# Moving the second block's activation low parts by 32 bytes inside their buffers

## The chip, the cores and the metric

The kernel runs on one core of a Trainium2 chip. The metric is device time in microseconds (us) of one execution, from the first instruction of any engine to the last. Five engines work side by side from queues of their own and wait for each other by semaphores: TensorE (PE in the profile; its weight loads are listed apart as PEld), VectorE (DVE), ScalarE (ACT), GpSimd (POOL) and SyncE (SP, which here issues most of the weight transfers). Operands of the matrix multiply lie in the on-chip memory SBUF, 128 partitions wide; an address in this text is the byte offset within a partition, the same on all partitions.

## The reference, cut to what matters

The program computes two model blocks, one after the other, on 512 tokens of width 1024, in float32.

```python
x = first_block(x, ...)    # gated MLP mixer, RWKV mixer, 32 experts (top 2), RMS norm
x = second_block(x, ...)   # two layers, below

for i in range(2):
    mix = ssd_shortconv_layer_mixer(x, ...) if i == 0 else sliding_window_attention(x, ...)
    x = layer_norm(ALPHA * x + mix, ...)
    x = layer_norm(ALPHA * x + (silu(x @ w_gate[i]) * (x @ w_up[i])) @ w_down[i], ...)
    x = x + (p[i] @ w_ple[i]) * sigmoid(x @ w_ple_gate[i] + b[i])
```

The feed-forward width is 2816. The change touches the second block alone, and in it every product of a weight matrix with the activations.

## The kernel before, in words

**Three products for one.** A float32 number is split into a high part in the rounded float32 format F32R, which the multiplier takes in one pass, and a low part, the rest, in the same format. `split` (lines 285 to 288) makes the parts of an activation: ACT copies the source to `xh` (line 287), DVE subtracts and writes `xl` (line 288). `conv` (lines 254 to 261) does the same for a weight tile: ACT writes `whi`, DVE `wlo`. `mm3` (lines 278 to 283) then issues three matrix multiplies into one PSUM tile: `whi` with `xh` (line 281), `whi` with `xl` (line 282), `wlo` with `xh` (line 283). The first named is the stationary operand, loaded 128 columns at a time before each multiply; the second is the moving operand, streamed through.

**Tiling.** Activations lie transposed: 128 of the 1024 (or 2816) channels on the partitions, the 512 tokens along the free dimension. So a moving operand is one row of 512 float32 numbers, 2,048 bytes in a partition, or, where a layer norm is worked in two halves of the tokens (`HALVES`, line 1426), 256 numbers. A stationary operand is 128 numbers, 512 bytes. `linear` (line 290) runs over the output groups of 128 columns and, inside, over the 8 (or 6, 16) channel groups k, three multiplies each. A weight tile of 1,024 numbers per partition is loaded by SP, split by ACT and DVE, and used; seven such buffers of each part rotate.

**Where the activation parts live.** In the second block, pool `act` (line 1488) has four buffers of the tile `xh` and four of `xl`. `four` (lines 1491 and 1492) takes one of each; each holds four channel groups, 4 x 512 numbers. `pair` (lines 1494 to 1498) hands out one channel group's `xh` and `xl` at a time. An activation of 1024 channels therefore fills two `xl` tiles: channel groups 0 to 3 in one, 4 to 7 in another.

The pool lays the buffers of one name one after the other. The built program has the four `xh` buffers at 94,848, 103,040, 111,232 and 119,424 and the four `xl` buffers at 127,616, 135,808, 144,000 and 152,192: all a whole number of times 128. The second block's weight tiles lie at whole multiples of 128 too (4,096 bytes each), and so do the stationary pieces, in steps of 512 bytes.

**Order.** TensorE executes its instructions in program order. The order around the change is set by the program text and by a tile framework that inserts the waits; nothing in it depends on addresses. In the second block come, in this order: the state-space mixer with its short convolution (lines 1506 to 1772), the feed-forward layer and gate of layer 0 (`ffn_ple`, line 1825), the attention of layer 1 (lines 1893 to 2007), and `ffn_ple` again.

Other products matter for comparison. The experts (`lin`, lines 1277 to 1283) have the roles swapped: the weights `whi` and `wlo` are the moving operand, 512 wide, and the activations `exh` and `exl` the stationary one, 96 columns (384 bytes) each, one after the other in their tile. The small product for `dt` (lines 1600 to 1607) uses 16 stationary columns (64 bytes) at a time.

Of the kernel before, what the change touches and what calls it, by code (L numbers as in the profile page):

```python
# [11 lines left out]
F32R = mybir.dt.float32r  # L12
# [8 lines left out]
T = 512  # L21
# [1455 lines left out]
def second(K, out, dbg=None):  # L1477
# [10 lines left out]
    act = es.enter_context(tc.tile_pool(name="act", bufs=4, reuse_waits="tile"))  # L1488
    spare = []

    def four():
        return tuple(act.tile([128, 4, T], F32R, name=n_) for n_ in ("xh", "xl"))

    def pair():
        if not spare:
            h_, l_ = four()
            spare.extend((h_[:, i_], l_[:, i_]) for i_ in range(4))
        return spare.pop(0)
# [15 lines left out]
    for b in range(4):  # L1514
        nc.sync.dma_start(ys[b], K.yd[b * 128:(b + 1) * 128, :])
    bcw = [cols(w, j) for w in (group(2048), group(2304)) for j in range(2)]
    x4 = [four() for _ in range(2)]
    x3 = [(h_[:, i_], l_[:, i_]) for h_, l_ in x4 for i_ in range(4)]
    bc_ps = [K.mm() for _ in range(4)]
# [384 lines left out]
    for b in range(4):  # L1904
        ps = K.mm()
        bs = slice(b * 128, (b + 1) * 128)
        for k in range(DC):
            xh, xl = xs[k]
# [128 lines left out]
```

## Time and profile before

| what | value |
|---|---|
| time, median of 3 runs | 2478.95 us (2475.49 to 2479.7) |
| the profiled execution: its own time | 2484.5 us |
| the profiled execution: its span, first to last instruction | 2482.6 us |
| TensorE busy | 2390.5 us, 96% of the span |
| VectorE busy | 1618.2 us, 65% |
| ScalarE busy | 1135.6 us, 46% |
| mean granted TensorE clock | 0.986 of full speed |

How to read it. The profile's page gives busy time by engine and by group of instructions. A matrix multiply is listed with its start and a duration of about 0.39 us for 512 columns; since the next one starts before the last has drained, durations overlap, and it is the distance between starts that says how long TensorE takes for one. That distance is called the spacing below. The timeline lists starts in us with two decimals, so that a spacing is best taken over many: the last start less the first, divided by the number of steps between. The granted clock is 1.00 where TensorE runs at 2.4 GHz and 0.5 where it runs at 1.2 GHz.

### The profile page before, as it was taken

The numbers are of one execution on the slowest core, as the hardware profiler recorded it, in microseconds if no ns is written. First come the engines' busy times: TensorE is split into PE (matmuls) and PEld (weight loads), VectorE is DVE, ScalarE is ACT, GpSimd is POOL, SyncE is SP. The second block draws the span as 40 slices with busy tenths as digits, with TensorE's granted clock in tenths as the row PEclk, the third lists the DMA queues.
The fourth block names the chain that finished last, engine by engine and source line by source line (L and its number), as shares of the span: only waits on it lengthen the run. The fifth ranks groups of instructions, "written<-read, shape, count | busy, mean of one in ns | idle before, by whom it ended". The sixth has DMA issues, their size and how long they took to land.

```text
span 2482.6 us, 36164 instructions
## 1 busy us (share of the span) xinstructions
PE 2390.5 (96%) x14570; PEld 1872.2 (75%) x14570; DVE 1618.2 (65%) x2543; ACT 1135.6 (46%) x1452; POOL 231.8 (9%) x73
## 2 busy tenths in 40 slices
PE   7999999799999999889999999999999998999998
PEld 3788677576666666568878898888888678888887
DVE  4778775699999999866766473333394677333346
ACT  2633324577677777564335333232353654223233
POOL 0000000112334444400000000000000000000000
PEclk9999999899999999989999999999999999999999
DMA  7233334799999999672323323322333112323232
GB/s 250 90 108 109 102 101 176 288 353 354 361 359 359 357 356 359 235 242 86 119 80 113 124 94 102 97 91 92 102 107 107 35 35 86 102 85 109 91 98 69
DMA packets 187307, 408.39 MB, mean 164 GB/s; under 512 B 13408, under 2 KB 130704, under 8 KB 162560
## 3 DMA queue, kind: packets, MB, share of 16 engines
q1 hardware_dynamic: 175840, 383.00, 44.2%
q0 software_dynamic: 5536, 10.46, 1.8%
q10 hardware_dynamic: 5760, 12.59, 1.4%
q8 instruction: 115, 1.88, 0.3%
q14 instruction: 56, 0.46, 0.0%
HBM read 389.17 MB, written 25.21 MB: 167 GB/s over the span
## 4 chain that ended last, share of the span: by engine, by line
PE 52%; DMA 17%; DVE 3%; issue 3%; ACT 1%; POOLq 0%; SPq 0%; DVEq 0%; ACTq 0%
PE mm L282 16%; PE mm L281 16%; PE mm L283 16%; DMA yd<-ey,r 15%; PE sc L1969 1%; PE po L1977 1%; PE pt L1946 1%; DMA raw<-in_w_mix_dram 1%; DVE x L1471 1%; DVE wlo L260 1%; DVE x L1472 0%; DMA s_row<-ard 0%; PE aux L1715 0%; DVE x L1473 0%; DVE xl L288 0%
## 5 line engine op out<-in xcount | busy, mean ns | idle before, releaser
L260 DVE TENSOR_TENSOR wlo<-raw,whi 128x1024 fp32r<-128x1024 f32 (+3 forms) x461 | 756.2, 1652 | 259.5 <-ACT whi L259 258.9
L281 PE MATMUL mm<-xh,whi 128*128 128x512 f32 (+1 forms) x2264 | 833.4, 370 | 17.5 <-ACT xh L287 6.8
L259 ACT ACTIVATE whi<-raw 128x1024 fp32r<-128x1024 f32 (+3 forms) x461 | 637.4, 1403 | 463.2 <-PE mm L282 374.7
L282 PE MATMUL mm<-xl,whi 128*128 128x512 f32 (+1 forms) x2264 | 832.7, 368 | 2.1 <-DVE xl L288 1.8
L283 PE MATMUL mm<-xh,wlo 128*128 128x512 f32 (+1 forms) x2264 | 831.2, 368 | 0.6 <-DVE wlo L260 0.6
L281 PEld LDWEIGHTS mm<-xh,whi 128*128 128x128 f32 x2264 | 427.2, 190 | 96.3 <-issue 9.4
L282 PEld LDWEIGHTS mm<-xl,whi 128*128 128x128 f32 x2264 | 430.3, 190 | 72.5 <-DVE xl L288 4.0
L283 PEld LDWEIGHTS mm<-xh,wlo 128*128 128x128 f32 x2264 | 429.7, 190 | 72.5 <-issue 5.2
L1344 POOL DMA_INDIRECT yd<-ey,r x32 | 210.9, 6590 | 380.7 <-DVE ey L1343 375.8
L1283 PE MATMUL mm<-wlo,exh 128*96 128x512 f32 x496 | 198.0, 401 | 12.1 <-DVE wlo L260 12.0
L1281 PE MATMUL mm<-whi,exh 128*96 128x512 f32 x496 | 197.0, 397 | 4.8 <-ACT exh L287 2.7
L1282 PE MATMUL mm<-whi,exl 128*96 128x512 f32 x496 | 195.8, 395 | 0.0
L1841 DVE TENSOR_TENSOR l_h<-l_sg,mm 128x512 f32<-128x512 f32 x44 | 30.2, 688 | 182.6 <-PE mm L283 167.0
L1283 PEld LDWEIGHTS mm<-wlo,exh 128*96 128x96 f32 x496 | 80.4, 162 | 56.9 <-DVE wlo L260 23.3
L1281 PEld LDWEIGHTS mm<-whi,exh 128*96 128x96 f32 x496 | 80.9, 163 | 38.0 <-ACT whi L259 3.0
L1282 PEld LDWEIGHTS mm<-whi,exl 128*96 128x96 f32 x496 | 80.6, 162 | 35.1
L1282 PE MATMUL aux<-whi,ehl 128*96 128x512 f32 x256 | 100.6, 394 | 0.8 <-DVE ehl L288 0.8
L1281 PE MATMUL aux<-whi,ehh 128*96 128x512 f32 x256 | 100.6, 393 | 0.0
L1283 PE MATMUL aux<-wlo,ehh 128*96 128x512 f32 x256 | 98.4, 400 | 0.0
L287 ACT ACTIVATE xh<-l_h 128x512 fp32r<-128x512 f32 x44 | 27.2, 623 | 111.7 <-DVE l_h L1841 111.7
L1840 ACT ACTIVATE l_sg<-mm 128x512 f32<-128x512 f32 x44 | 25.8, 589 | 83.1 <-PE mm L283 83.0
L1282 PEld LDWEIGHTS aux<-whi,ehl 128*96 128x96 f32 x256 | 41.3, 161 | 19.3 <-DVE ehl L288 1.2
(570 smaller groups left out, 2546.4 us busy)
## 6 DMA issues: line engine op xcount, KB each, us to landing
raw<-in_moe_gate_dram SPq DMA_DIRECT2D x64, 1024.0 KB, 7.5
raw<-in_moe_up_dram SPq DMA_DIRECT2D x64, 1024.0 KB, 7.4
raw<-in_moe_down_dram SPq DMA_DIRECT2D x64, 1024.0 KB, 8.6
raw<-in_w_mix_dram SPq DMA_DIRECT2D x44, 512.0 KB, 3.5
raw<-in_w_ffn_gate_dram SPq DMA_DIRECT2D x44, 512.0 KB, 3.5
raw<-in_w_ffn_up_dram SPq DMA_DIRECT2D x44, 512.0 KB, 3.5
raw<-in_w_ffn_down_dram SPq DMA_DIRECT2D x40, 512.0 KB, 3.3
raw<-in_ada_w_dram SPq DMA_DIRECT2D x64, 256.0 KB, 2.7
```

The lines of the kernel that those rows point to most:

```text
L259: nc.scalar.activation(hi[:, :m], r[:, :m], AF.Copy)
L260: nc.vector.tensor_tensor(lo[:, :m], r[:, :m], hi[:, :m], op=OP.subtract)
L281: nc.tensor.matmul(ps, h, xh, start=start, stop=False)
L282: nc.tensor.matmul(ps, h, xl, start=False, stop=False)
L283: nc.tensor.matmul(ps, l, xh, start=False, stop=stop)
L287: self.nc.scalar.activation(xh, src, AF.Copy)
L1281: nc.tensor.matmul(ps, xh[:, k, :], wh, start=(k == 0), stop=False)
L1282: nc.tensor.matmul(ps, xl[:, k, :], wh, start=False, stop=False)
L1283: nc.tensor.matmul(ps, xh[:, k, :], wl, start=False, stop=(k == len(ww) - 1))
L1344: nc.gpsimd.indirect_dma_start(out=yd, out_offset=bass.IndirectOffsetOnAxis(ap=yi, axis=0), in_=y, in_offset=None, bounds_check=T - 1, oob ...
L1840: nc.scalar.activation(sg, pp["g", j], AF.Silu)
L1841: V.tensor_tensor(h, sg, pp["u", j], op=OP.mult)
```

## The change

Each `xl` tile gets 8 more numbers (32 bytes) per partition, and the part that is used begins behind them. Nothing else is edited; the `xh` tiles stay as they are.

```diff
     def four():
-        return tuple(act.tile([128, 4, T], F32R, name=n_) for n_ in ("xh", "xl"))
+        h_ = act.tile([128, 4, T], F32R, name="xh")
+        return h_, act.tile([128, 4 * T + 8], F32R, name="xl")[:, 8:].rearrange("p (i n) -> p i n", i=4)
```

What comes out in the built program: each `xl` buffer is now 8,224 bytes instead of 8,192, and the pool still puts them end to end, starting at 127,616. The buffers begin at 127,616, 135,840, 144,064 and 152,288, and what is used in them begins 32 bytes later: at 127,648, 135,872, 144,096 and 152,320. Modulo 128 that is 32, 64, 96 and 0. All tiles allocated above them move up by 4 x 32 = 128 bytes and keep their place modulo 128. `xh`, the weight tiles and everything below stay where they were. No engine gets another instruction, and none is moved. Of the 1,544 multiplies of the second block that stream an `xl` of 512 columns, 484 find it at 32 modulo 128, 272 at 64, 312 at 96 and 476 at 0; of the 544 that stream 256 columns, 144, 160, 112 and 128. In 16 multiplies (line 1912) a piece of `xl` off 0 modulo 128 is the stationary operand.

## Rows read from the trace of the kernel before

**Rows 1.** The page's first part: busy us, share of the span and number of instructions of an engine.

```profile
PE 2390.5 (96%) x14570; PEld 1872.2 (75%) x14570; DVE 1618.2 (65%) x2543; ACT 1135.6 (46%) x1452; POOL 231.8 (9%) x73
```

**Rows 2.** Busy time of each engine in stretches of the span: from 1080 us (about where the second block's products begin) to the end, and the gate and up and down products of the two feed-forward layers. Columns: stretch, its length, then for each engine busy us and instructions, the granted clock, the DMA engines' busy share and their GB/s.

```profile
1080.00:2482.60 1402.60, 1376.29 (x7172) 1145.29 (x7172) 755.68 (x1470) 522.03 (x839) 2.53 (x7) 0.99 0.30 95
1468.00:1789.00 321.00, 320.78 (x1457) 267.29 (x1456) 119.04 (x134) 89.63 (x110) 0.00 (x0) 1.00 0.32 102
2076.00:2397.00 321.00, 321.00 (x1463) 267.77 (x1462) 117.60 (x136) 89.81 (x110) 0.00 (x0) 1.00 0.30 96
```

**Rows 3.** The groups of TensorE's instructions from 1079.5 us to the end, different widths kept apart: line, operation, out<-in, shape, count, busy us and mean ns of one, and the idle time before them.

```profile
L282 PE MATMUL mm<-xl,whi 128*128 128x512 f32 x1536 | 601.0, 391 | 0.0
L283 PE MATMUL mm<-xh,wlo 128*128 128x512 f32 x1536 | 600.9, 391 | 0.0
...
L282 PE MATMUL mm<-xl,whi 128*128 128x256 f32 x544 | 156.3, 290 | 2.1 <-DVE xl L288 1.8
L283 PE MATMUL mm<-xh,wlo 128*128 128x256 f32 x544 | 155.2, 288 | 0.0
```

**Rows 4.** The timeline of TensorE, 512 columns, in a long undisturbed sequence: start us, length, line, tiles. The last row shown is the 24th start after the first.

```profile
1339.33 0.39 PE L281 MATMUL mm<-xh,whi 128*128 128x512 f32 x1
1339.56 0.39 PE L282 MATMUL mm<-xl,whi 128*128 128x512 f32 x1
1339.78 0.39 PE L283 MATMUL mm<-xh,wlo 128*128 128x512 f32 x1
...
1344.77 0.39 PE L281 MATMUL mm<-xh,whi 128*128 128x512 f32 x1
```

**Rows 5.** The same for 256 columns; the last row is the 26th start after the first.

```profile
1438.23 0.28 PE L281 MATMUL mm<-xh,whi 128*128 128x256 f32 x1
...
1441.35 0.28 PE L283 MATMUL mm<-xh,wlo 128*128 128x256 f32 x1
```

**Rows 6.** The timeline of TensorE just behind a foreign product (line 1765, two plain float32 multiplies) that broke into a sequence of 512 columns. The row at 1348.36 is the 9th start after the one at 1346.28, the one at 1349.72 the 6th after that.

```profile
1345.12 1.10 PE L1765 MATMUL aux<-s_v,cst_c 128*128 128x512 f32 x2
1345.65 0.79 PE L282 MATMUL mm<-xl,whi 128*128 128x512 f32 x1
1346.28 0.39 PE L283 MATMUL mm<-xh,wlo 128*128 128x512 f32 x1
1346.51 0.40 PE L281 MATMUL mm<-xh,whi 128*128 128x512 f32 x1
1346.74 0.40 PE L282 MATMUL mm<-xl,whi 128*128 128x512 f32 x1
1346.98 0.39 PE L283 MATMUL mm<-xh,wlo 128*128 128x512 f32 x1
1347.20 0.39 PE L281 MATMUL mm<-xh,whi 128*128 128x512 f32 x1
...
1348.36 0.39 PE L283 MATMUL mm<-xh,wlo 128*128 128x512 f32 x1
...
1349.72 0.39 PE L283 MATMUL mm<-xh,wlo 128*128 128x512 f32 x1
```

**Rows 7.** The same for 256 columns, behind a layer norm's two products (line 1457). The row at 1444.65 is the 7th start after the one at 1443.83.

```profile
1443.20 0.67 PE L1457 MATMUL aux<-l_q,cst_c 128*128 128x256 f32 x2
...
1443.83 0.28 PE L282 MATMUL mm<-xl,whi 128*128 128x256 f32 x1
...
1444.65 0.28 PE L283 MATMUL mm<-xh,wlo 128*128 128x256 f32 x1
```

**Rows 8.** The timeline of TensorE in the experts, 512 moving columns, 96 stationary ones. The last row is the 23rd start after the first.

```profile
706.17 0.39 PE L1281 MATMUL mm<-whi,exh 128*96 128x512 f32 x1
706.40 0.39 PE L1282 MATMUL mm<-whi,exl 128*96 128x512 f32 x1
...
711.51 0.40 PE L1281 MATMUL mm<-whi,exh 128*96 128x512 f32 x1
```

**Rows 9.** The timeline of TensorE in the product for `dt`, 512 moving columns, 16 stationary ones. The last row is the 20th start after the first.

```profile
1107.50 0.40 PE L281 MATMUL mm<-xh,wdh 128*16 128x512 f32 x1
...
1112.14 0.40 PE L283 MATMUL mm<-xh,wdl 128*16 128x512 f32 x1
```

**Rows 10.** Two lines of plain float32 products with 512 moving columns: count, duration in ns (least, median, most), first and last start, form. The moving tile `s_xde` lies at 64 modulo 128 in the built program, `o_sq` at 96.

```profile
L1726 PE MATMUL aux<-s_xde,s_bt x12: 590/592/697, 1196.8 to 1289.6; 128*128 128x512 f32 x12
L808 PE MATMUL aux<-o_sq,cst_c x8: 590/592/697, 220.3 to 375.3; 128*128 128x512 f32 x8
```

**Rows 11.** DVE's writes of the low parts of the feed-forward activations (line 288), and a DVE operation of the same width whose output `s_so` lies at 64 modulo 128 (line 1677); columns as in rows 10.

```profile
L288 DVE TENSOR_TENSOR xl<-l_h,xh x44: 681/686/694, 1481.2 to 2394.3; 128x512 fp32r<-128x512 f32 x44
L1677 DVE TENSOR_TENSOR s_so<-mm,s_so x8: 691/692/693, 1174.8 to 1313.0; 128x512 f32<-128x512 f32 x8
```

## The prediction

> **What bounds the kernel now.** I read the page's first part first: TensorE is busy 96% of the span, no other engine over 65% [rows 1]. Then the table by stretches: from 1080 us to the end TensorE is busy 1376.3 of 1402.6 us, and in the two feed-forward stretches practically all of 321 us each, at a granted clock of 1.00, while VectorE and ScalarE are at little over a third and a quarter and the DMA engines at 0.3 [rows 2]. So in the second block the time is the number of multiplies times the distance between their starts; a nanosecond more or less on each is paid in full but for the 26.3 us (2%) in which TensorE idles. The groups of TensorE give the numbers: 1,536 low-part products of 512 columns and 544 of 256, each one of a triple [rows 3].
>
> The spacing is therefore the thing to read. In a long sequence 24 steps take 1344.77 - 1339.33 = 5.44 us, 226.7 ns each [rows 4]; with 256 columns 26 steps take 3.12 us, 120.0 ns each [rows 5]. The difference is 106.7 ns for 256 columns, which is one column per period at 2.4 GHz. So 512 columns stream in 213.3 ns, 256 in 106.7, and in both cases 13.3 ns are added: exactly the time of 32 columns, or 128 bytes of the moving operand. A remainder that is the same for both widths and just 128 bytes long smells of a memory that is served in turns of 128 bytes.
>
> Two more readings say that this remainder is not fixed. Behind a foreign product the spacing first wanders between 0.22 and 0.24 us: 9 steps take 2.08 us, 231.1 ns each; only then does it settle, 6 steps in 1.36 us, 226.7 ns [rows 6]. With 256 columns the unsettled spacing is shorter: 7 steps in 0.82 us, 117.1 ns [rows 7]. And it never settles in the experts, where the stationary pieces are 384 bytes and so begin alternately at even and odd multiples of 128: 23 steps in 5.34 us, 232.2 ns [rows 8]; nor in the small product with stationary pieces of 64 bytes: 20 steps in 4.64 us, 232.0 ns [rows 9]. The settled 226.7 ns is thus found where every operand begins at the same place modulo 512 from one multiply to the next. The three unsettled values, 231.1, 232.2 and 232.0, have the mean 231.8.
>
> [...]
>
> **The change part by part.** Removed: nothing. Added: no instruction, no wait, no transfer; the order on every queue is the same. Moved: addresses.
>
> Tiles above the pool shift by 128 bytes and keep their place modulo 128; I cost that at nothing. DVE's writes of `xl` now begin off a multiple of 128: at 0 modulo 128 they take 686 ns in the median, a like operation with its output at 64 takes 692 [rows 11]. Six ns on the 44 writes of rows 11 are 0.3 us, on all low parts of the block well under 1 us, on an engine busy 755.7 of 1402.6 us [rows 2]: nothing. If that cover were gone it would still be under 1 us.
>
> What counts is the moving operand of line 282. The title's place, 32 modulo 128, holds for one of the four buffers only; the others are at 64, 96 and 0. So 1,068 of the low-part products of 512 columns are shifted and 476 are not; of those of 256 columns 416 and 128. No row shows an F32R stream that begins off a multiple of 128, so the cost is bounded from both sides. Upwards: the shifted product and its two neighbours never settle, and the spacing goes from 226.7 to 231.8 ns, 5.1 ns for each multiply. Downwards: the remainder of one multiply per triple vanishes, 13.3 ns less.
>
> I take the unsettled value, since rows 8 and 9 are nearest: there, too, one operand begins at a changing place, and the spacing stays high. The sum:
> - 512 columns: 1,068 shifted triples x 3 = 3,204 multiplies x 5.1 ns = +16.3 us.
> - 256 columns: 416 x 3 = 1,248 multiplies x (117.1 - 120.0 = -2.9 ns) = -3.6 us.
> - Triples with `xl` at 0 stand among shifted ones: a product over 8 channel groups takes 12 multiplies from one tile and 12 from the next, and settling takes 9 (rows 6). So up to three quarters of them stay unsettled: 476 x 3 x 0.75 x 5.1 ns = +5.5 us, less 128 x 3 x 0.75 x 2.9 ns = 0.8 us.
>
> That is +12.7 us without the last item and +17.4 us with all of it. A few of these multiplies are unsettled already, behind foreign products, and some fall where TensorE idles anyway, so I stay near the lower end: +14 us. A second way to the same size: if starts are bound to turns of 128 bytes, a shift of 64 makes the way there 16 columns longer than a whole turn and the way back too, 48 + 48 + 32 instead of 32 + 32 + 32, which is 32 columns or 13.3 ns per triple; on 1,068 triples +14.2 us. The profiled execution took 2484.5 us, which would become 2498.5; it lies 5.5 us above the median of the runs, 2478.95. On that median the forecast is 2493.
>
> **The rivals.**
>
> Nothing happens. Plain float32 products of 512 columns have the same least and median duration, 590 and 592 ns, whether their moving tile lies at 64 or at 96 modulo 128 [rows 10]. If F32R streams are as indifferent, the spacing stays at 226.7 and 120.0 ns and the time at 2479, between 2474 and 2484. Against it: the same remainder reacts to where stationary pieces begin [rows 8, 9], and a float32 product of 512 columns takes 590 ns where an F32R one takes 391 [rows 3], so that its memory has more time for each column. [...] Chance 0.27.
>
> Faster: the turns help. If the next stream may begin as soon as its own turn comes and needs less than 8 columns of a gap, then going from `xh` to a shifted `xl` and back costs one turn of 32 columns together where it now costs two. Each shifted triple loses 13.3 ns: (1,068 + 416) x 13.3 = -19.8 us, 2459. It speaks for it that the remainder is 32 columns for either width. Against it: among 512 columns no spacing in rows 6 is under 0.22 us, while this needs 0.217 regularly. It decides from the point where a shift of 8 columns is enough for the gap. This is the case on the other side. Chance 0.17.
>
> Slower by much more: not only the shifted triples but all 1,536 of 512 columns stay unsettled, 4,608 x 5.1 = +23.5 us, and the 256 wide ones gain nothing: 2502. It is the upper end of the forecast's own range, not a case apart.
>
> That the change does not do what it says is built in: three of the four buffers lie elsewhere than at 32. Were it the 32 alone that matters, only 484 of the 512 wide triples would pay, 484 x 3 x 5.1 = +7.4 us, 2486, the lower end of the forecast's own range.
>
> **How the numbers follow.** Slower by unsettled streams 0.56 (own range 2486 to 2504), nothing 0.27, faster 0.17. What a measurement of this kernel can tell from no change is about 0.2%, 5 us; the case "nothing" lies within it, so the three chances are the same three numbers. The range that leaves out the faster case and a little of the upper tail goes from 2473 to 2504.
>
> **What will show it.** In the timeline of the feed-forward stretches, 512 columns: a spacing averaged over 24 starts of about 231 to 232 ns says that the forecast's step is right, 226.7 the first rival, about 222 the second. With 256 columns: 117 against 120 ns. The counts of all engines and the DMA rows should be as before, and the granted clock 1.00 in these stretches. I am wrong if the two stretches of 321 us are not longer; if they are longer by about 3 us each, the step is right, since their 1,457 instructions are some 485 triples [rows 2] of which 69% are shifted (1,068 of 1,544): 485 x 0.69 x 3 x 5.1 ns = 5.1 us each, and 3 us if a good third of them settle. It would also be wrong if the time came from elsewhere, say from longer `xl` writes on VectorE that TensorE waits for.

## The result and the profile after

The changed kernel takes 2498.67 us in the median of 4 runs (2495.5 to 2502.66), the kernel before 2478.34 in the same comparison: a ratio of 1.0085, 95% interval 1.0072 to 1.0099, so 20.3 us more (18 to 25 by the interval). The profiled execution after took 2499.61 us, its span is 2497.7 us.

The page's first part after, against [rows 1]: the same number of instructions on every engine, 16 us more in TensorE's multiplies, 6 us less in its weight loads (PEld), under 1 us of difference elsewhere.

```profile
PE 2406.9 (96%) x14570; PEld 1866.6 (75%) x14570; DVE 1617.5 (65%) x2543; ACT 1135.3 (45%) x1452; POOL 231.6 (9%) x73
```

The stretches of [rows 2] after (stretch, its length, then busy us and instructions of each engine, granted clock, DMA share, GB/s): TensorE is as busy and its clock as high as before, but in 321 us of the first feed-forward layer it gets through 1,424 instructions where it was 1,457, and VectorE and ScalarE do less beside it, since they work at TensorE's pace. The third stretch lies at the same times as before, but the wide multiplies of the second layer now begin 7 us later in it (2094.44 against 2087.43 us), behind more of the narrow ones, so its count is nearly the same.

```profile
1080.00:2497.70 1417.70, 1389.90 (x7127) 1135.66 (x7125) 752.03 (x1465) 517.48 (x830) 1.55 (x2) 1.00 0.30 93
1468.00:1789.00 321.00, 320.28 (x1424) 260.98 (x1423) 115.52 (x130) 87.45 (x106) 0.00 (x0) 1.00 0.31 96
2076.00:2397.00 321.00, 321.00 (x1460) 263.05 (x1460) 118.29 (x148) 87.38 (x109) 0.00 (x0) 1.00 0.31 93
```

TensorE's groups after, against [rows 3] (line, operation, out<-in, shape, count, busy us and mean ns of one, idle time before them). Both views begin at 1079.5 us; the second block begins earlier in this trace, and some 14 of its triples of 256 columns fall before the view, which is why their counts are lower. The mean duration of the wide multiplies rises by 3 to 5 ns, that of the narrow ones falls by 4: the two widths answer with opposite signs.

```profile
L282 PE MATMUL mm<-xl,whi 128*128 128x512 f32 x1536 | 608.8, 396 | 0.0
L283 PE MATMUL mm<-xh,wlo 128*128 128x512 f32 x1536 | 605.7, 394 | 0.0
L282 PE MATMUL mm<-xl,whi 128*128 128x256 f32 x530 | 150.5, 286 | 1.2 <-DVE xl L288 1.1
L283 PE MATMUL mm<-xh,wlo 128*128 128x256 f32 x531 | 149.2, 284 | 0.0
```

The starts say it exactly. Two timelines of TensorE follow (start us, length, line, tiles), six rows of each kernel at the same places of the program: the first multiply of the `dt` product, the first and the last of the 1,416 multiplies of 512 columns that run without a break through the feed-forward layer of layer 0, two of 256 columns right behind them that are 72 steps apart, and the last multiply of all. Before:

```profile
1106.49 0.41 PE L281 MATMUL mm<-xh,wdh 128*16 128x512 f32 x1 [1.00 <-ACT wdh L287]
...
1478.66 0.50 PE L281 MATMUL mm<-xh,whi 128*128 128x512 f32 x1 [0.22 <-ACT l_sg L1840]
...
1799.55 0.39 PE L283 MATMUL mm<-xh,wlo 128*128 128x512 f32 x1
1799.78 0.28 PE L281 MATMUL mm<-xh,whi 128*128 128x256 f32 x1
...
1808.41 0.28 PE L281 MATMUL mm<-xh,whi 128*128 128x256 f32 x1
...
2476.93 0.39 PE L283 MATMUL mm<-xh,wlo 128*128 128x512 f32 x1
```

After:

```profile
1100.21 0.41 PE L281 MATMUL mm<-xh,wdh 128*16 128x512 f32 x1 [1.72 <-ACT wdh L287]
...
1478.93 0.50 PE L281 MATMUL mm<-xh,whi 128*128 128x512 f32 x1 [0.72 <-ACT l_sg L1841]
...
1807.21 0.39 PE L283 MATMUL mm<-xh,wlo 128*128 128x512 f32 x1
1807.44 0.28 PE L281 MATMUL mm<-xh,whi 128*128 128x256 f32 x1
...
1815.89 0.27 PE L281 MATMUL mm<-xh,whi 128*128 128x256 f32 x1
...
2492.04 0.40 PE L283 MATMUL mm<-xh,wlo 128*128 128x512 f32 x1
```

From the `dt` product to the last multiply: 2476.93 - 1106.49 = 1370.44 us before, 2492.04 - 1100.21 = 1391.83 after, 21.4 more. (In the profiled execution after, the `dt` product begins 6.3 us earlier. The second block's very first multiply already begins 6.5 us earlier, 1072.65 against 1079.14, so the difference lies in the first block, which the change doesn't touch; that is why the two spans differ by 15.1 only.) In the undisturbed sequence 1,415 steps took 320.89 us and take 328.28: 226.8 and 232.0 ns. The 72 steps of 256 columns took 8.63 us and take 8.45: 119.9 and 117.4 ns.

To split the 21.4 us I took all starts of the trace and joined them with the addresses in the built program, and averaged over whole triples (of 256 columns those without a wait). The mean ns per multiply:

| place of `xl`, modulo 128 | 512 columns | 256 columns |
|---|---|---|
| before, all at 0 | 226.84 | 119.87 |
| after, at 32 | 231.74 | 118.00 |
| after, at 64 | 232.09 | 118.28 |
| after, at 96 | 231.31 | 118.07 |
| after, at 0 | 233.15 | 117.46 |

The 1,068 shifted triples of 512 columns lie at 231.70 in the weighted mean, 4.86 ns over before: 3,204 x 4.86 = +15.6 us. The 476 at 0 lie 6.31 over: 1,428 x 6.31 = +9.0 us. With 256 columns the shifted ones save 1,248 x 1.74 = 2.2 us, the others 384 x 2.41 = 0.9. That is +21.5 us, the 21.4 of the starts. So close an agreement is partly chance: in the kernel before and the four experiments below whose spacing settles, the way from the `dt` product to the last multiply takes 1367.3 to 1370.9 us.

The plain float32 product of [rows 10], line 1727 now, has kept its duration (count, least/median/most ns, first and last start). Its moving tile has moved by 128 bytes, but its stationary tile by the same 128, so their distance is the multiple of 256 that it was, and this says nothing on the distance. The lines of rows 10 do: the operands of line 808 lie 96 bytes apart modulo 256, those of line 1726 a multiple of 256, at the same duration. But each of these is one pair of passes, 428 to 430 or 533 to 535 ns from start to start, with microseconds between the pairs, and no long sequence.

```profile
L1727 PE MATMUL aux<-s_xde,s_bt x12: 590/592/697, 1192.3 to 1287.1; 128*128 128x512 f32 x12
```

### The profile page after: what moved, and what is told of

It reads as the page before. It is cut to its first block, busy times and chain, and to the rows that moved or that the text cites. A ratio compares the mean times of both kernels' runs of the same rounds, so it can differ in the third digit from the quotient of the medians.

```text
span 2497.7 us, 36164 instructions
## 1 busy us (share of the span) xinstructions
PE 2406.9 (96%) x14570; PEld 1866.6 (75%) x14570; DVE 1617.5 (65%) x2543; ACT 1135.3 (45%) x1452; POOL 231.6 (9%) x73
## 4 chain that ended last, share of the span: by engine, by line
PE 52%; DMA 16%; DVE 4%; issue 3%; ACT 1%; POOLq 0%; another core or an unknown queue 0%; DVEq 0%; POOL 0%; SPq 0%; ACTq 0%
PE mm L281 16%; PE mm L282 16%; PE mm L283 16%; DMA yd<-ey,r 15%; PE sc L1970 1%; PE po L1978 1%; PE pt L1947 1%; DVE x L1471 1%; DVE wlo L260 1%; DVE x L1472 0%; DMA s_row<-ard 0%; DVE x L1473 0%; DVE xl L288 0%; PE aux L1716 0%; PE aux L1718 0%
## 5 line engine op out<-in xcount | busy, mean ns | idle before, releaser
L1797 DVE SCALAR_TENSOR_TENSOR x<-x,mm 128x512 f32<-128x512 f32 (+1 forms) x26 | 16.8, 645 | 60.4 <-PE mm L283 60.4
```

## The experiments

Two things stood out: the spacing is high where the prediction had it high, and it is highest at the place that counts as unshifted. So what sets it? The candidates were the place itself (off a multiple of 128), the change of place from one moving operand to the next, turns of 128 bytes, and the distance between the moving and the stationary operand. The program has four kinds of operands in the second block, `xh`, `xl`, `whi` and `wlo`; in the kernel before all of them begin at 128 modulo 256. Each experiment moves some kinds by a fixed number of bytes with an unused tile in front of the buffers (filled up behind them, so that what lies above keeps its place modulo 128; the fills `gc` behind `xl` and `gg` behind `whi` are left out below); the instructions and their order stay. All computation stays too.

The edits have one form; shown are 8 unused columns of 4 bytes, 32 bytes, in every place where an experiment may have them.

```diff
+    es.enter_context(tc.tile_pool(name="ga", bufs=1)).tile([128, 8], F32, name="ga")
     act = es.enter_context(tc.tile_pool(name="act", bufs=4, reuse_waits="tile"))
+    es.enter_context(tc.tile_pool(name="gb", bufs=1)).tile([128, 8], F32, name="gb")
+    acl = es.enter_context(tc.tile_pool(name="acl", bufs=4, reuse_waits="tile"))
...
-        return tuple(act.tile([128, 4, T], F32R, name=n_) for n_ in ("xh", "xl"))
+        return act.tile([128, 4, T], F32R, name="xh"), acl.tile([128, 4, T], F32R, name="xl")
```

`ga` moves `xh` and `xl`, `gb` moves `xl` alone. For the weights the same is done in front of the second block's buffers, `gd` for `wlo` and `gf` for `whi`; `ge` fills up behind `wlo`, so that the pools that follow keep their places modulo 512 (`pad` opens a pool with one unused tile of so many columns, in the second block alone):

```diff
+        pad("gd", 8)
         los = [pool("lop", b) for b in lo]
+        pad("ge", 120)
         self.raw = pool("raw", raw)
+        pad("gf", 8)
         self.groups = [(pool("hip", b), l) for b, l in zip(hi, los)]
```

Of each run one view is shown: the timeline of TensorE, first and last of the same 1,416 multiplies, 1,415 steps apart.

**All four `xl` buffers at 32** (`gb` of 8 columns, no `ga`): what the change's title says, for every buffer.

> All four xl buffers begin at 32 modulo 128 (and modulo 512 at the same place as each other); xh and weights as before. Alternation theory (a sequence settles only when the moving operand begins at the same place from one multiply to the next): nothing settles, 231 to 233 ns per 512-column multiply, time about 2499 us, as with the change. Turns of 128 bytes: 40 + 56 + 32 columns per triple, 231.1 ns, about 2498 to 2503. Rival 'only 32 helps and the other places hurt': 222 ns per multiply, about 2459 us.

```profile
1479.27 0.50 PE L281 MATMUL mm<-xh,whi 128*128 128x512 f32 x1 [0.57 <-ACT l_sg L1843]
...
1809.54 0.39 PE L283 MATMUL mm<-xh,wlo 128*128 128x512 f32 x1
```

Measured 2500.6 against 2477.45 us, ratio 1.0086 (1.0069 to 1.0103); 330.27 us for the 1,415 steps, 233.4 ns each. All at 32 costs what the mixture of the change costs; the mixture is no cause of its own.

**`xh` and `xl` both 32 up** (`ga` of 8).

> xh and xl buffers all begin at 32 modulo 128, weights as before. Alternation theory: successive moving operands begin at the same place again, so the sequences settle at 226.7 and 120.0 ns and the time is that of before, 2479 us. Off-the-line theory (a moving operand that begins off a multiple of 128 costs by itself): all three multiplies of a triple pay, over 232 ns each, 2505 us or more. Against-the-weights theory (the place of the moving operand relative to the stationary one decides): not 226.7 ns, about 232, 2499 us.

```profile
1478.38 0.50 PE L281 MATMUL mm<-xh,whi 128*128 128x512 f32 x1 [0.64 <-ACT l_sg L1843]
...
1808.64 0.40 PE L283 MATMUL mm<-xh,wlo 128*128 128x512 f32 x1
```

Measured 2503.95 us, ratio 1.0111 (1.0094 to 1.0128), 233.4 ns. Here every moving operand begins at the same place modulo 512 as the one before it, and the spacing doesn't settle. That the place changes from one multiply to the next is therefore not what the change pays for.

**`xl` 128 up** (`gb` of 32): a whole turn, if there are turns of 128 bytes.

> All four xl buffers are moved by 128 bytes, so that xl and xh begin at the same place modulo 128 but 128 apart modulo 256. If the place modulo 128 is what counts: settled, 226.7 ns, 2479 us. If it is the place modulo 256 (as the experts' stationary pieces of 384 bytes suggest): never settled, about 232 ns, 2499 us.

```profile
1478.42 0.50 PE L281 MATMUL mm<-xh,whi 128*128 128x512 f32 x1 [0.53 <-ACT l_sg L1842]
...
1805.55 0.40 PE L283 MATMUL mm<-xh,wlo 128*128 128x512 f32 x1
```

Measured 2494.32 us, ratio 1.0065 (1.0048 to 1.0082), 231.2 ns. A move by a multiple of 128 cost 4.4 ns a multiply here: turns of 128 bytes fall.

**`whi` and `wlo` 32 up, no activation moved** (`gd` and `gf` of 8).

> The weight tiles whi and wlo of the second block begin at 32 modulo 128, xh and xl as before. Alternation theory: the moving operands still begin at one place, the stationary ones too, so 226.7 and 120.0 ns and 2479 us. Against-the-weights theory: the two are 32 bytes apart, as in the run with both activation parts moved, so it gives the same as that run, about 232 ns and 2499 us. Off-the-line theory: nothing for a moving operand; 2479 unless the stationary operand pays, too.

```profile
1481.95 0.50 PE L289 MATMUL mm<-xh,whi 128*128 128x512 f32 x1 [0.60 <-ACT l_sg L1848]
...
1812.21 0.40 PE L291 MATMUL mm<-xh,wlo 128*128 128x512 f32 x1
```

Measured 2507.95 us, ratio 1.0125 (1.0108 to 1.0142), 233.4 ns: as much as any move of activations, although each moving operand lies where it lay, modulo 512. The stationary operand's place has a share in these 233.4 ns. So the next runs moved both kinds.

**`xh` and `xl` both 64 up** (`ga` of 16).

> xh and xl buffers all begin 64 bytes further, weights as before. Against-the-weights theory (a sequence settles only where moving and stationary operand begin at the same place modulo 128 or more): unsettled as with 32, about 233 ns per 512-column multiply and 2503 us. Rival, turns of 64 bytes: settled, 226.7 ns, 2479 us.

```profile
1475.04 0.50 PE L281 MATMUL mm<-xh,whi 128*128 128x512 f32 x1 [0.59 <-ACT l_sg L1843]
...
1799.05 0.39 PE L283 MATMUL mm<-xh,wlo 128*128 128x512 f32 x1
```

Measured 2484.91 against 2478.61 us, ratio 1.0029 (1.0016 to 1.0042), 229.0 ns. That is a third of the way from settled to worst, not the 233 ns of the expectation; the time follows the spacing.

**`xh` and `xl` both 128 up** (`ga` of 32).

> xh and xl buffers all begin 128 bytes further, weights as before. If moving and stationary operand must agree modulo 128: settled, 226.7 ns, 2478 us. If modulo 256: unsettled, 230 to 233 ns, 2492 to 2505 us. The run with xl alone moved by 128 was slower by 0.65%; this tells whether that came from xl against xh (then this one is settled) or from xl against the weights (then it is not).

```profile
1479.02 0.50 PE L281 MATMUL mm<-xh,whi 128*128 128x512 f32 x1 [0.48 <-ACT l_sg L1842]
...
1809.28 0.39 PE L283 MATMUL mm<-xh,wlo 128*128 128x512 f32 x1
```

Measured 2500.86 us, ratio 1.0088 (1.0071 to 1.0105), 233.4 ns. Every operand begins at a multiple of 128 and like its neighbours; still not settled.

**`xh` and `xl` both 256 up** (`ga` of 64).

> xh and xl buffers all begin 256 bytes further, so that they agree with the weights modulo 512 where they lay 256 apart before. Against-the-weights theory with any period up to 256: settled, 226.7 and 120.0 ns, 2478 us. With a period of 512: another value, settled or not. It is also the control for the fill that moves the tiles above.

```profile
1474.67 0.50 PE L281 MATMUL mm<-xh,whi 128*128 128x512 f32 x1 [0.41 <-ACT l_sg L1842]
...
1795.55 0.39 PE L283 MATMUL mm<-xh,wlo 128*128 128x512 f32 x1
```

Measured 2480.06 us, ratio 1.0003 (0.9993 to 1.0013), 226.8 ns: settled.

**All four kinds 32 up** (`ga`, `gd` and `gf` of 8). Nothing lies at a multiple of 128 any more.

> xh, xl, whi and wlo of the second block all begin 32 bytes further. Against-the-weights theory: only the distance counts, and it is that of before, so 226.7 and 120.0 ns and 2478 us. Off-the-line theory (a place off a multiple of 128 costs by itself): slower than either part alone, 2508 us or more, or at least about 2500.

```profile
1475.09 0.50 PE L289 MATMUL mm<-xh,whi 128*128 128x512 f32 x1 [0.39 <-ACT l_sg L1851]
...
1795.96 0.39 PE L291 MATMUL mm<-xh,wlo 128*128 128x512 f32 x1
```

Measured 2478.94 us, ratio 1.0004 (0.9994 to 1.0014), 226.8 ns. Either half of this edit alone costs 26 to 31 us; together they cost nothing that shows. So the place as such made no difference at 32 bytes, and how moving and stationary operands lie to each other made one of 6.6 ns a multiply. With 256 columns the mean is 119.9 ns again, against 116.9 where `xh` and `xl` alone are 32 up.

**All four kinds 128 up**, the same trial with the 128 bytes that cost 22 us on the activations alone (`ga`, `gd` and `gf` of 32).

> High and low activation parts and both weight parts of the second block all 128 bytes up. Theory of the distance (a multiply streams without extra only where the byte distance from its stationary to its moving operand is a multiple of 256): the distance is the old one, so 226.7 ns between starts and 2479 us, although the same 128 bytes on the activations alone cost 22 us. Rival, the place itself (the moving operand must begin at a multiple of 256 counted from its old place): 232.8 ns and 2500 us as with the activations alone.

```profile
1474.58 0.50 PE L289 MATMUL mm<-xh,whi 128*128 128x512 f32 x1 [0.28 <-ACT l_sg L1850]
...
1795.45 0.39 PE L291 MATMUL mm<-xh,wlo 128*128 128x512 f32 x1
```

Measured 2478.18 against 2478.47 us, ratio 0.9995 (0.9986 to 1.0004), 226.8 ns.

**`xl` alone 256 up** (`gb` of 64).

> Only the low activation parts, 256 bytes up, the high parts stay. Theory of the distance modulo 256: 226.7 ns and 2479 us, the kernel before. Rival, a distance that must be the same modulo 512 for all three multiplies of a triple: 229 to 232 ns and 2491 to 2502 us, like 128 bytes on the low parts (2494).

```profile
1471.20 0.50 PE L281 MATMUL mm<-xh,whi 128*128 128x512 f32 x1 [0.61 <-ACT l_sg L1842]
...
1792.07 0.39 PE L283 MATMUL mm<-xh,wlo 128*128 128x512 f32 x1
```

Measured 2478.95 us, ratio 1.0003 (0.9994 to 1.0012), 226.8 ns. A distance longer by 256 gave the spacing of before, and moving operands that differ by 256 from each other settled.

**`wlo` alone 32 up** (`gd` of 8): one multiply of three has another distance.

> Only the low weight parts, 32 bytes up; every activation part and the high weight parts stay. One multiply of three has another distance. Theory of the distance: that is enough, the whole triple leaves 226.7 ns for an average between 229 and 233 ns, 2490 to 2504 us, although no moving operand lies anywhere else than before. Rival, only the place of moving operands counts: 226.7 ns and 2479 us.

```profile
1478.11 0.50 PE L287 MATMUL mm<-xh,whi 128*128 128x512 f32 x1 [0.24 <-ACT l_sg L1846]
...
1808.38 0.39 PE L289 MATMUL mm<-xh,wlo 128*128 128x512 f32 x1
```

Measured 2503.76 us, ratio 1.0111 (1.0095 to 1.0126), 233.4 ns. One unlike distance in a triple was enough to lift the mean of the three from 226.8 to 233.4 ns.

**`xl` and `wlo` 32 up, the high parts not** (`gb` and `gd` of 8). The last question was which pair meets. The trace of the kernel before shows each weight load (PEld) beside the multiply ahead of the one it is for: `wlo` is loaded while `xl` streams, `whi` while `xh` does.

```profile
1340.23 0.39 PE L282 MATMUL mm<-xl,whi 128*128 128x512 f32 x1
1340.24 0.19 PEld L283 LDWEIGHTS mm<-xh,wlo 128*128 128x128 f32 x1
...
1340.46 0.39 PE L283 MATMUL mm<-xh,wlo 128*128 128x512 f32 x1
1340.46 0.19 PEld L281 LDWEIGHTS mm<-xh,whi 128*128 128x128 f32 x1
```

If the load and the stream beside it disturbed each other by their distance, this edit would leave both pairs as they were.

> Low activation parts and low weight parts both 32 bytes up, the high parts stay. Each of the two moves alone costs 23 to 25 us. Theory of the pair that meets in time (what counts is the moving operand of the running multiply against the stationary operand that is loaded beside it for the next one: xh beside whi, xl beside wlo): both pairs keep their old distances, so 226.7 ns and 2479 us. Theory of the pair of one multiply (whi with xh, whi with xl, wlo with xh): two of three multiplies have a new distance, 229 to 234 ns and 2490 to 2506 us.

```profile
1478.85 0.50 PE L287 MATMUL mm<-xh,whi 128*128 128x512 f32 x1 [0.80 <-ACT l_sg L1849]
...
1807.55 0.39 PE L289 MATMUL mm<-xh,wlo 128*128 128x512 f32 x1
```

Measured 2500.38 against 2479.99 us, ratio 1.0082 (1.0068 to 1.0096), 232.3 ns. The pair that meets in time is not the whole rule, plausible as the timeline made it look. All twelve runs agree with this: the spacing settled where the byte distance from each multiply's stationary operand to its own moving one is a multiple of 256 (226.8 ns in layer 0 of all four such runs), and nowhere else (229.0 to 233.4 ns in layer 0 of the other eight). For these three products that says the same as: all four kinds lie alike modulo 256, since `whi` with `xh`, `whi` with `xl` and `wlo` with `xh` link all four. Other links would do so too, for example the pairs that meet in time together with moving operands that agree with each other. Which pairs make the extra time is therefore not shown.

## Why the prediction was right, and where it was not

**What bounds the kernel** held. TensorE is the limit of the second block, the counts, the transfers and the clock are as before, and the time went where the prediction sent it, into the spacing. VectorE's writes of `xl` take no longer (684 ns in the median after, for the 44 of [rows 11]), and the 1,416 multiplies take 7.4 us longer in layer 0 and 7.9 us in layer 1, so nothing has to be looked for elsewhere.

**The unsettled value** held: 231.8 ns was taken from [rows 6, 8, 9] for the shifted triples, 231.70 is what they show. That term was +16.3 and is +15.6 us. That it fits to 0.1 ns is partly luck: the value was borrowed from streams with other distances, and unlike distances give 228.9 to 233.4 ns in the experiments; with 64 bytes on both activation parts it is 229.0, and the time rises by 6.3 us only.

**The term that failed** is the item "Triples with `xl` at 0 stand among shifted ones", which let up to three quarters of them stay unsettled at the same 231.8, and after it the choice "I stay near the lower end". They were sized at +5.5 us and, with +14 between +12.7 and +17.4, taken by about a quarter; they measure +9.0, the highest spacing of all, 233.15 ns. The reason is not that settling takes 9 starts. "1,068 of the low-part products of 512 columns are shifted and 476 are not" counted the fourth buffer, at 152,320, as unmoved, because it is at 0 modulo 128. It has moved by 128 bytes, its distance to the weights is no longer a multiple of 256, and the run with `xl` alone 128 up shows that this distance doesn't settle either (231.2 ns in layer 0): the modulus was wrong. With this item in full and at its size the sum is the +21.5 us above. For the same reason a feed-forward layer lengthens by 7.4 to 7.9 us instead of 5.1: all its triples pay, not 69% of them. So +14 us was forecast and +20.3 came. The range, 2473 to 2504, held it, but it held the case of no change as well; what bears the forecast out is the spacing.

**The term for 256 columns** had the right sign and was too large: -3.6 and -0.8 us forecast, -2.2 and -0.9 measured, since 117.1 ns was read from 7 steps [rows 7] and the long mean of the shifted ones is 118.1.

**The reason** given was half right. "One operand begins at a changing place" named a condition that the runs refute: `xh` and `xl` both 32 up have no changing place and do not settle (233.4 ns), `xl` alone 256 up has one and does (226.8 ns). The second way, turns of 128 bytes, came to the same size by chance and falls with the 128-byte runs (231.2 ns with `xl` moved, 233.4 with `xh` and `xl`). What [rows 8, 9] have in common with the change is the distance: with stationary pieces 384 or 64 bytes apart against moving operands in steps of 2,048 it is a multiple of 256 only for every second or fourth piece. That this keeps those two streams at 232.2 and 232.0 ns is argued from their addresses; no run moved them.

**The rivals.** "Nothing happens" rested on plain float32 products of one duration at two places. Those are single pairs of passes 428 to 535 ns apart, whose distance the change left as it was, so they say little of a long stream at 227 ns; the step from them to F32R was what failed. Nor is the moving operand's place all that counts: moving only the weights by 32 bytes costs 1.25%, and moving all four kinds costs nothing that shows (a ratio of 1.0004). "Faster" needed 222 ns; layer 0's sequence of 1,416 is under 226.7 in none of the kernels. Only with 256 columns does the unlike distance save something, 1 to 3 ns each (116.9 to 118.7 ns against 119.9), far too little here.

## What to carry to other kernels

Where F32R multiplies with 512 moving columns follow one another back to back, look at the byte distance between stationary and moving operand modulo 256, not at the alignment of either one: in this kernel, at a granted clock of 1.00, the spacing was 226.7 ns with all operands alike and 229 to 233 with any other distance tried (32, 64, 96 and 128 bytes). Whether it is so elsewhere no run here shows. A pad in or in front of one buffer shifts every buffer behind it, also those that look unmoved by the modulus one has in mind, so read the addresses of the built program before counting which operands changed. And a spacing read from first and last start of a thousand multiplies settles within 0.1 ns what a whole-kernel time can only show with many runs. Read more than one sequence, though: two of the same kernel can differ by 2 ns, as the next section shows.

## What the runs showed of the hardware that was not expected

The spacing falls into few values. A column's time is taken here from [rows 4, 5], where 256 columns more take 106.7 ns at a granted clock of 1.00, 2.4 columns per ns. Where the granted clock was 0.50, from 1064.34 to 1066.90 us of the trace before, six steps of F32R multiplies of 512 columns took 2.56 us, 426.7 ns each or 1.2 columns per ns; the 2.4 and 1.2 GHz ahead are these rates, counted as one column per period. Settled, the spacing is 226.7 ns, 544 columns' time, in all five kernels with like distances. The highest is 233.4 ns (233.3 without the longer first step), 560 columns' time, the same to 0.1 ns in layer 0's sequence of 1,416 for five different edits (32 on `xl`, on `xh` and `xl`, on `whi` and `wlo`, on `wlo` alone, 128 on `xh` and `xl`). 64 bytes give 229.0, between the two. Three others, each with several distances, stand in between: 231.2 (128 on `xl`), 232.0 (the changed kernel) and 232.3 (32 on both low parts).

In these runs the distances told whether a sequence settles, but not alone which of the higher values it takes. With all four `xl` buffers at 32, each kind of operand keeps one place modulo 512 through the whole block. Yet layer 0's 1,416 multiplies stand 233.4 ns apart there, and layer 1's, whose first and last are shown here, 327.02 us over 1,415 steps, 231.1 ns:

```profile
2096.40 0.40 PE L281 MATMUL mm<-xh,whi 128*128 128x512 f32 x1
...
2423.42 0.39 PE L283 MATMUL mm<-xh,wlo 128*128 128x512 f32 x1
```

With `xl` 128 up the two layers have 231.2 and 228.9, with `xh` and `xl` 128 up 233.4 and 232.4. What chooses between them stays open.

A high mean is not noise either. The start times of the trace show short cycles that repeat: 229, 232, 239 ns again and again with `wlo` alone 32 up, 229 and 238 in turn with `xh` and `xl` 128 up in layer 0. Three starts in a row take 680 ns where the spacing is settled and 686.7, 693.3 or 700.0 at 228.9, 231.1 and 233.3 ns, so these values are 6.67 ns per triple apart, 16 columns' time. What in the chip makes the cycles stays open; that in these runs a sequence settled with the distances modulo 256 alike (226.8 ns) and not otherwise (228.9 to 233.4) is shown, the mechanism behind it is not.

Over the 213.3 ns of 512 columns at that rate, the spacing of these F32R streams was 13.4 ns more (226.7 less 213.3) at the best and 20.1 (233.4 less 213.3) at the worst.
